# Stick-breaking sums as a VectorE scan, and probabilities and values turned on VectorE and ScalarE

## The chip, the cores and the metric

The kernel runs on one core of a Trainium2 chip. The metric is the device time of one execution in microseconds (us), less being better. The core has a matrix engine (TensorE, PE), two elementwise engines with 128 lanes (VectorE, DVE, and ScalarE, ACT), GpSimd (POOL) and a sync engine (SP) that issues most DMA transfers. Each engine works through its own instructions in a fixed order and waits for the others by semaphores.

## The reference

A two-layer decoder trunk on 272 tokens (16 learned meta tokens and 256 input tokens), 2048 features, 16 heads of 128. Layer 0 is forgetting attention, layer 1 stick-breaking attention; each is followed by a squared-ReLU MLP with 8192 hidden features.

```python
# layer 0, forgetting attention, for a block of queries qs:qe
s = einsum(q[qs:qe], k[:qe]) * scale + cum_logf[q] - cum_logf[k]
p = softmax(where(k_pos <= q_pos, s, -inf))
o = einsum(p, v[:qe])
# layer 1, stick-breaking attention
z = einsum(q[qs:qe], k[:qe]) * scale
mask = k_pos < q_pos
log_beta = log_sigmoid(z)
log_one_minus = where(mask, log_sigmoid(-z), 0.0)
suffix = cumsum(log_one_minus, reverse=True) - log_one_minus
a = where(mask, exp(log_beta + suffix), 0.0)
o = einsum(a, v[:qe])
# both: h = h + o @ w_o ; h = h + square(relu(rms_norm(h) @ w_up)) @ w_down
```

## The kernel before

Activations are feature-major: 16 chunks of 128 features on the partitions, tokens along the free axis. Every matrix product with weights goes through `gemm_group`: 512 output features as four blocks m of 128 with one accumulator each, and four steps kb of 512 input features. Precision comes from splitting: a weight block arrives by DMA in two halves of 128x1024 (`raw`), ACT rounds a half to `whi` (L229), DVE writes the rest to `wlo` (L230), and PE makes three products for each block, hi·hi, lo·hi and hi·lo (L182), 48 matmuls in a kb step. `raw`, `whi` and `wlo` have four buffers each, so that the halves are made up to two kb steps ahead. Steps kb 0 and 3 run block m by block m and read both halves from the start; steps 1 and 2 run half by half.

Each attention works on four groups g of four heads. In layer 0 a group has a q GEMM, a k GEMM, scores and softmax, a v GEMM and outputs; in layer 1 the q GEMMs of all groups come first. Scores are float32 products that PE makes in several passes (`ps` L401; `pza`, `pzb` L579 and L580). In layer 0, queries are on the partitions, so that the probabilities have to be turned before the outputs: PE transposes them (`pp` L432 to L434), DVE copies them. In layer 1, keys are on the partitions, and the running sums over keys are products with triangular and all-ones matrices (`pta`, `ptb` L594 to L599; a corner of 16 queries apart, `pzc`, `ptc`). In both layers PE transposes the values (`token_major`, `pv` L334). The outputs `po` are split into `ao` by ACT and DVE (`put_split`, L355 and L356), which `out_proj` reads.

The program is scheduled: the framework orders each engine's instructions by a simulated timeline, within the data's dependences. Only the order of the GEMM's own matmuls is pinned (`gemm_matmul`).

Of the kernel before, what the change touches and what calls it, by code (L numbers as in the profile page):

```python
# [34 lines left out]
def yoco_kernel(ctx: ExitStack, tc: tile.TileContext, hT_in, gains, b_f, w_f, w_qkv0, w_o0, w_up, w_dn,  # L35
# [25 lines left out]
    for _ in range(9):  # L61
# [15 lines left out]

# [15 lines left out]
    maskB = const.tile([P, 400], F32, name="maskB")  # L93
    nc.gpsimd.memset(maskB, 0.0)
    nc.gpsimd.affine_select(out=maskB[:, 0:256], in_=maskB[:, 0:256], compare_op=ALU.is_gt, fill=-BIG,
                            base=M, pattern=[[1, 256]], channel_multiplier=-1)
    nc.gpsimd.affine_select(out=maskB[:, 256:400], in_=maskB[:, 256:400], compare_op=ALU.is_gt, fill=-BIG,
                            base=0, pattern=[[1, 144]], channel_multiplier=-1)

    maskC = const.tile([P, 4, M], F32, name="maskC")  # L100
    nc.gpsimd.memset(maskC, 0.0)
    nc.gpsimd.affine_select(out=maskC, in_=maskC, compare_op=ALU.is_gt, fill=-BIG, base=M,
                            pattern=[[32, 4], [1, M]], channel_multiplier=-1)
    nc.gpsimd.affine_select(out=maskC, in_=maskC, compare_op=ALU.is_ge, fill=-BIG, base=-M,
                            pattern=[[-32, 4], [0, M]], channel_multiplier=1)
# [9 lines left out]
    pad = align.tile([P, 32], F32, name="pad")  # L115
# [64 lines left out]
    def gemm_matmul(*args, **kw):  # L180

        ins = nc.tensor.matmul(*args, **kw).ins  # L182
# [101 lines left out]
    def load_gates():  # L284
        nc.scalar.dma_start(bf_sb, b_f)

        wf_sb = att.tile([P, NC, NC], F32, tag="v_sb", name="wf_sb")
        wf = att.tile([P, NC, 2 * NC], F32R, tag="v_sb", name="wf")
# [3 lines left out]
        both = att.tile([P, P], F32, tag="pk", name="both")[:2 * NC, :NC]  # L292
# [36 lines left out]
    def token_major(vT, pr, t0, label):  # L329

        pv = patt.tile([P, 2, 2, P], F32, tag="patt", name=f"pv_{label}")
        for i in range(2):
            for b in range(2):
                nc.tensor.transpose(pv[:, i, b, :], vT[:, 2 * pr + i, t0 + b * P:t0 + b * P + P], ident)  # L334
        v_sb = att.tile([P, 2, 2, P], F32, tag="v_sb", name=f"v_sb_{label}")
        nc.scalar.copy(v_sb, pv)
        return v_sb

    def packed(src, label):

        n = src.shape[2]
        t = att.tile([P, P], F32, tag="pk", name=f"pk_{label}")[:, :4 * n]
        nc.gpsimd.tensor_copy(t.rearrange("p (h t) -> p h t", h=4), src)
        return t

    def corners(a, b, label):

        t = att.tile([P, P], F32, tag="pk", name=f"pk_{label}")
# [9 lines left out]
    ao = Split("o0", 0)  # L358
    for g in range(4):
        qT = att.tile([P, 4, T], F32, tag="qT", bufs=4, name=f"qT0_{g}")  # L360
        kT = att.tile([P, 4, T], F32, tag="kT", bufs=1, name=f"kT0_{g}")
        vT = att.tile([P, 4, T], F32, tag="vT", bufs=1, name=f"vT0_{g}")
# [4 lines left out]

        def evac_kv(m, acc, t):
            nc.vector.tensor_tensor(out=t[:, m, :], in0=acc, in1=box["rstd"], op=ALU.mult)
# [14 lines left out]
        s = att.tile([P, 4, 416], F32, tag="s", bufs=1, name=f"s_{g}")  # L384

        def decays(j):

            for i, (o, n) in enumerate(((0, 144), (144, T))):
# [4 lines left out]
        gemm_group(w_qkv0[3 * g + 1], xa, 0, lambda m, acc: evac_kv(m, acc, kT),  # L393
                   after={j: (lambda j=j: decays(j)) for j in range(4)})


        for j in range(4):
            h = 4 * g + j
            ps = patt.tile([P, 512], F32, tag="patt", name=f"ps_{h}")
            for q0, o, n in ((M, 0, 144), (M + P, 144, T)):  # L400
                nc.tensor.matmul(ps[:, o:o + n], qT[:, j, q0:q0 + P], kT[:, j, :n], start=True, stop=True)  # L401
# [13 lines left out]
        s0 = att.tile([P, P], F32, tag="s0", name=f"s0_{g}")  # L415
# [10 lines left out]
        pps = []  # L426
        for pr in range(2):
            pp_sb = att.tile([P, 2, 416], F32, tag="pp", bufs=3, name=f"pp_sb_{g}_{pr}")
            for i in range(2):
                j = 2 * pr + i  # L430
                pp = patt.tile([P, 512], F32, tag="patt", name=f"pp_{4 * g + j}")
                nc.tensor.transpose(pp[:, 0:P], s[:, j, 0:P], ident)  # L432
# [3 lines left out]
            pps.append(pp_sb)  # L436


        pm = patt.tile([P, 512], F32, tag="patt", name=f"pm_{g}")
        nc.tensor.transpose(pm[:, 0:P], corners(s[:, :, P:144], s[:, :, 400:416], f"sm_{g}"), ident)  # L440
        nc.tensor.transpose(pm[:, P:2 * P], s0, ident)
        pm_sb = att.tile([P, 256], F32, tag="pm_sb", bufs=1, name=f"pm_sb_{g}")
        nc.vector.tensor_tensor(out=pm_sb[:, :P].rearrange("p (b q) -> p b q", q=M), in1=maskD, op=ALU.mult,
                                in0=pm[:, P - M:P].unsqueeze(1).to_broadcast([P, 8, M]))
        nc.scalar.copy(pm_sb[:, P:], pm[:, P:2 * P])

        gemm_group(w_qkv0[3 * g + 2], xa, 0, lambda m, acc: evac_kv(m, acc, vT))

        pv = patt.tile([P, 512], F32, tag="patt", name=f"pvm_{g}")
        nc.tensor.transpose(pv[:, :P], packed(vT[:, :, 0:32], f"vm_{g}"), ident)
        nc.tensor.transpose(pv[:, P:2 * P], corners(vT[:, :, P:144], vT[:, :, 256:T], f"vc_{g}"), ident)
        vm_sb = att.tile([P, 2 * P], F32, tag="vm_sb", bufs=1, name=f"vm_sb_{g}")
        nc.scalar.copy(vm_sb, pv[:, :2 * P])
        po = patt.tile([P, 512], F32, tag="patt", name=f"pom_{g}")
        nc.tensor.matmul(po[:, :P], vm_sb[:, :P], pm_sb[:, P:], start=True, stop=True)
        put_split(ao, 4 * g, 4, 0, M, po[:, :P].rearrange("p (h q) -> p h q", h=4)[:, :, :M])
        for pr in range(2):
            v_sb = token_major(vT, pr, 0, f"0_{g}_{pr}")  # L460
            po = patt.tile([P, 2, 256], F32, tag="patt", name=f"po0_{g}_{pr}")
            for i in range(2):
                nc.tensor.matmul(po[:, i, :], v_sb[:, i, 0, :], pps[pr][:, i, 0:2 * P], start=i == 0, stop=False)  # L463
                nc.tensor.matmul(po[:, i, P:], v_sb[:, i, 1, :], pps[pr][:, i, 2 * P:3 * P], start=False, stop=False)  # L464
            nc.tensor.matmul(po.rearrange("p i (c q) -> p (i c) q", c=2)[:, :, P - M:], vm_sb[:, P:],
                             pm_sb[:, 64 * pr:64 * pr + 64], start=False, stop=True)
            put_split(ao, 4 * g + 2 * pr, 2, M, S, po)


    def out_proj(w, ao, t0, gi, label):  # L470
        norm = Norm(label, t0)
        xm = Split(label, t0)
        for g in range(4):
# [5 lines left out]
            gemm_group(w[g], ao, t0, evac, widen=t0 == M)  # L479
# [30 lines left out]
    xm, norm_m = out_proj(w_o0, ao, 0, G_M0, "m0")  # L510
# [30 lines left out]
    ao = Split("o1", M)  # L541
    for g in range(4):
        kT = att.tile([P, 4, T], F32, tag="kT", bufs=1, name=f"kT1_{g}")
        vT = att.tile([P, 4, T], F32, tag="vT", bufs=1, name=f"vT1_{g}")
        gemm_group(w_kv[2 * g], xc, 0, lambda m, acc: evac_kv(m, acc, kT))
        q = qT1[g]

        def softplus(e, z):

            nc.scalar.activation(e, z, AF.Abs)  # L550
            nc.scalar.activation(e, e, AF.Exp, scale=-1.0)
            nc.scalar.activation(e, e, AF.Ln, bias=1.0)
# [179 lines left out]
```

## Time and profile before

| What | Before |
|---|---|
| Time, median of 3 runs | 2303.12 us (2302.21 to 2303.5) |
| Profiled execution, its own time | 2303.47 us |
| Span of the profiled execution | 2301.7 us |
| PE busy | 2290.6 us (100%) |
| DVE busy | 1289.2 us (56%) |
| ACT busy | 1041.2 us (45%) |
| POOL busy | 41.5 us (2%) |
| Attention of layer 0, one group of heads | 80.12 us |
| Attention of layer 1, one group of heads | 56.87 us |

The span runs from the first to the last instruction of the profiled execution; its own time has 1.77 us around the span. A row of a group reads: line, engine, operation, written tile <- read tiles, shapes, count, then busy time, mean ns of one, and idle time just before them with what ended it. A row of a timeline or of the chain starts with start and length in us. A row of a stretch has its bounds, its length, and the busy time and count of each engine.

### The profile page before, as it was taken

What the parts mean: (1) busy time and instruction counts of PE and PEld (TensorE: products, weight loads), DVE (VectorE), ACT (ScalarE), POOL (GpSimd) and SP (SyncE); (2) the same over time, 40 slices, a digit from 0 to 9 for tenths busy, and PEclk for the clock granted to TensorE, in tenths of its full rate; (3) what the DMA queues carried; (4) which work ended last, traced back from release to release, by engine and by line L of the source; (5) the groups of instructions that cost most, each with busy time, mean ns of one, the idle gap of its engine ahead of it and who ended that gap; (6) DMA issues with size and microseconds to landing.
All of it is one profiled execution on the core that took longest, in us unless ns stands there. A gap on an engine that the chain in (4) does not pass through costs nothing.

```text
span 2301.7 us, 44826 instructions
## 1 busy us (share of the span) xinstructions
PE 2290.6 (100%) x19030; PEld 2282.9 (99%) x19030; DVE 1289.2 (56%) x1764; ACT 1041.2 (45%) x1397; POOL 41.5 (2%) x72
## 2 busy tenths in 40 slices
PE   9999999999999999999999999999999999999998
PEld 9999999999999999999999999999999999999998
DVE  7665555655455455455566555566555555555554
ACT  6444344543344344344444444455544543543553
POOL 1000000000000000000000000000000000000000
PEclk9999999999999999999999999999999999999999
DMA  7545555555555555555555544456556566566563
GB/s 235 164 161 173 163 168 166 173 184 172 185 175 176 182 174 184 173 184 174 178 189 186 173 147 147 148 173 201 187 192 201 189 190 203 186 197 199 186 202 129
DMA packets 116904, 412.32 MB, mean 179 GB/s; under 512 B 13520, under 2 KB 16992, under 8 KB 116704
## 3 DMA queue, kind: packets, MB, share of 16 engines
q1 hardware_dynamic: 114560, 406.29, 54.8%
q8 instruction: 149, 2.44, 0.4%
q10 hardware_dynamic: 2144, 3.17, 0.4%
q14 instruction: 51, 0.42, 0.1%
HBM read 407.29 MB, written 2.11 MB: 178 GB/s over the span
## 4 chain that ended last, share of the span: by engine, by line
PE 99%; DMA 1%; DVE 0%; ACT 0%; issue 0%; DVEq 0%; SPq 0%; ACTq 0%
PE acc L182 95%; DMA raw<-w_qkv 1%; PE ps L401 0%; PE pv L334 0%; PE pza L579 0%; PE po L463 0%; PE po L618 0%; PE pzb L580 0%; PE po L619 0%; PE po L464 0%; DMA hT<-hT_in 0%; DVE ob L674 0%; PE pf L301 0%; PE pf L300 0%; PE pta L594 0%; PE pta L595 0%
## 5 line engine op out<-in xcount | busy, mean ns | idle before, releaser
L230 DVE TENSOR_TENSOR wlo<-raw,whi 128x1024 fp32r<-128x1024 f32 (+1 forms) x773 | 929.0, 1218 | 742.7 <-ACT whi L229 736.2
L229 ACT ACTIVATE whi<-raw 128x1024 fp32r<-128x1024 f32 (+1 forms) x773 | 797.3, 1050 | 1010.8 <-PE acc L182 985.9
L182 PE MATMUL acc<-x_m,whi 128*128 128x272 f32 (+1 forms) x4096 | 643.2, 281 | 0.0
L182 PE MATMUL acc<-x_u,whi 128*128 128x272 f32 (+1 forms) x4096 | 642.9, 281 | 0.0
L182 PEld LDWEIGHTS acc<-x_m,whi 128*128 128x128 f32 x4096 | 566.1, 188 | 0.1
L182 PEld LDWEIGHTS acc<-x_u,whi 128*128 128x128 f32 x4096 | 565.9, 188 | 0.0
L182 PE MATMUL acc<-x_m,wlo 128*128 128x272 f32 (+1 forms) x2048 | 440.9, 281 | 0.0
L182 PE MATMUL acc<-x_u,wlo 128*128 128x272 f32 (+1 forms) x2048 | 440.8, 281 | 0.0
L182 PE MATMUL acc<-x_a,whi 128*128 128x272 f32 (+1 forms) x2048 | 360.5, 288 | 0.3 <-ACT whi L229 0.3
L182 PEld LDWEIGHTS acc<-x_m,wlo 128*128 128x128 f32 x2048 | 323.4, 188 | 0.0
L182 PEld LDWEIGHTS acc<-x_u,wlo 128*128 128x128 f32 x2048 | 323.3, 188 | 0.0
L182 PEld LDWEIGHTS acc<-x_a,whi 128*128 128x128 f32 x2048 | 302.3, 189 | 1.8 <-ACT whi L229 0.6
L182 PE MATMUL acc<-x_a,wlo 128*128 128x272 f32 (+1 forms) x1024 | 254.4, 286 | 0.0
L182 PE MATMUL acc<-x_kv,whi 128*128 128x272 f32 x1024 | 191.8, 288 | 0.0
L182 PEld LDWEIGHTS acc<-x_a,wlo 128*128 128x128 f32 x1024 | 175.9, 189 | 1.3 <-issue 0.5
L182 PE MATMUL acc<-x_o,whi 128*128 128x272 f32 (+1 forms) x1024 | 161.9, 282 | 0.0
L182 PEld LDWEIGHTS acc<-x_kv,whi 128*128 128x128 f32 x1024 | 159.7, 188 | 0.0
L182 PE MATMUL acc<-x_kv,wlo 128*128 128x272 f32 x512 | 147.5, 288 | 0.0
L182 PEld LDWEIGHTS acc<-x_o,whi 128*128 128x128 f32 x1024 | 141.7, 188 | 0.0
L259 DVE TENSOR_TENSOR hT<-acc,hT 128x272 f32<-128x272 f32 (+1 forms) x160 | 69.1, 432 | 84.7 <-PE acc L182 84.6
L182 PE MATMUL acc<-x_o,wlo 128*128 128x272 f32 (+1 forms) x512 | 110.5, 282 | 0.0
L182 PEld LDWEIGHTS acc<-x_kv,wlo 128*128 128x128 f32 x512 | 96.4, 188 | 0.0
(225 smaller groups left out, 974.4 us busy)
## 6 DMA issues: line engine op xcount, KB each, us to landing
raw<-w_up SPq DMA_DIRECT2D x256, 512.0 KB, 4.6
raw<-w_dn SPq DMA_DIRECT2D x256, 512.0 KB, 4.6
raw<-w_qkv SPq DMA_DIRECT2D x92, 512.0 KB, 4.0
raw<-w_o SPq DMA_DIRECT2D x64, 512.0 KB, 4.4
raw<-w_kv SPq DMA_DIRECT2D x64, 512.0 KB, 3.8
raw<-w_q SPq DMA_DIRECT2D x32, 512.0 KB, 4.9
fk<-f_dram ACTq DMA_DIRECT2D x4, 544.0 KB, 5.2
raw<-w_qkv SPq DMA_DIRECT2D x7, 256.0 KB, 4.8
```

The lines of the kernel that those rows point to most:

```text
L182: ins = nc.tensor.matmul(*args, **kw).ins
L229: on_act = nc.scalar.activation(hp, src, AF.Copy)
L230: on_dve = nc.vector.tensor_tensor(out=lp, in0=src, in1=hp.bitcast(F32), op=ALU.subtract)
L259: nc.vector.tensor_tensor(out=hT[:, c, t0:], in0=acc, in1=hT[:, c, t0:], op=ALU.add)
```

## The change

Scores of both layers now have queries on the partitions and are made by one function: a float32 product for the first 128 queries (144 keys), and three products of split parts for the other 128 (272 keys); queries are split once per group, keys at each eviction. In layer 1 the sums over keys become DVE scans along the free axis, and the corner is no longer computed apart. Probabilities of both layers are turned by two wide DVE transposes, which turn blocks of 32x32, and sixteen ACT copies that put the blocks in place (`turned`). Values are turned by sixteen DVE transposes of 32 partitions each, which write the blocks in place (`token_major`). The outputs of a group are made later, in two pieces (`late`): in layer 0 ahead of kb 2 of the next q GEMM and after that GEMM; in layer 1 ahead of kb 1 and kb 3 of the next k GEMM; for the last group ahead of kb 1 and kb 3 of `out_proj`'s first GEMM. Some buffers change their pools.

```diff
+    def behind(ins):
+        tc.add_manual_dep(ins.ins, queued[0].name, mybir.DependencyInfo(mybir.DependencyClass.NoSync,
+                                                                        mybir.DependencyReason.DATA))
...
+    def split_q(q, label):
+        parts = [att.tile([P, 4, P], F32R, tag="qs", name=f"q{x}_{label}") for x in ("h", "l")]
+        nc.scalar.activation(parts[0], q, AF.Copy)
+        nc.vector.tensor_tensor(out=parts[1], in0=q, in1=parts[0].bitcast(F32), op=ALU.subtract)
+        return parts
+    def keys(label):
...
+        def evac(m, acc):
+            nc.vector.tensor_tensor(out=kT[:, m, :], in0=acc, in1=box["rstd"], op=ALU.mult)
+            nc.scalar.activation(kh[:, m, :], kT[:, m, :], AF.Copy)
+            nc.vector.tensor_tensor(out=kl[:, m, :], in0=kT[:, m, :], in1=kh[:, m, :].bitcast(F32), op=ALU.subtract)
+    def scores(q, qs, kT, ks, j, label):
+        ps = patt.tile([P, 512], F32, tag="patt", name=f"ps_{label}_{j}")
+        nc.tensor.matmul(ps[:, :144], q[:, j, :], kT[:, j, :144], start=True, stop=True)
+        for i, (a, b) in enumerate(((0, 0), (0, 1), (1, 0))):
+            nc.tensor.matmul(ps[:, 144:416], qs[a][:, j, :], ks[b][:, j, :], start=i == 0, stop=i == 2)
+        return ps
+    def turned(s, label):
...
+        for o, u, n in ((0, 0, P), (144, P, 2 * P)):
+            nc.vector.transpose(out=sb.rearrange("p (h k) -> p h k", h=4)[:, :, u:u + n], in_=s[:, :, o:o + n])
+        sb, out = (t.rearrange("p (u k) -> p u k", k=P) for t in (sb, pt))
+        for a in range(4):
+            for b in range(4):
+                nc.scalar.activation(out[32 * b:32 * b + 32, :, 32 * a:32 * a + 32],
+                                     sb[32 * a:32 * a + 32, :, 32 * b:32 * b + 32], AF.Copy)
-    def token_major(vT, pr, t0, label):
-        pv = patt.tile([P, 2, 2, P], F32, tag="patt", name=f"pv_{label}")
-        for i in range(2):
-            for b in range(2):
-                nc.tensor.transpose(pv[:, i, b, :], vT[:, 2 * pr + i, t0 + b * P:t0 + b * P + P], ident)
-        v_sb = att.tile([P, 2, 2, P], F32, tag="v_sb", name=f"v_sb_{label}")
-        nc.scalar.copy(v_sb, pv)
+    def token_major(vT, label):
+        vt = att.tile([P, 4, T], F32, tag="kv", name=f"vt_{label}")[:, :, :2 * P]
+        out, src = (t.rearrange("p h (b t) -> p h b t", t=P) for t in (vt, vT[:, :, :2 * P]))
+        for a in range(4):
+            for b in range(4):
+                nc.vector.transpose(out=out[32 * b:32 * b + 32, :, :, 32 * a:32 * a + 32],
+                                    in_=src[32 * a:32 * a + 32, :, :, 32 * b:32 * b + 32])
...
@@ layer 0
-            gemm_group(w_qkv0[3 * g], xa, 0, evac_q)
+            gemm_group(w_qkv0[3 * g], xa, 0, evac_q, {2: late[0]})
+        qs = split_q(qT[:, :, M + P:], f"0_{g}")
+        for f in late[1:]:
+            f()
...
-            for i in range(2):
-                j = 2 * pr + i
-                pp = patt.tile([P, 512], F32, tag="patt", name=f"pp_{4 * g + j}")
-                nc.tensor.transpose(pp[:, 0:P], s[:, j, 0:P], ident)
-                nc.tensor.transpose(pp[:, P:2 * P], s[:, j, 144:144 + P], ident)
-                nc.tensor.transpose(pp[:, 2 * P:3 * P], s[:, j, 144 + P:144 + 2 * P], ident)
-                nc.vector.tensor_copy(pp_sb[:, i, :3 * P], pp[:, :3 * P])
+        sm = corners(s[:, :, P:144], s[:, :, 400:416], f"sm_0_{g}")
+        probs = turned(s, f"0_{g}")
+        vT, evac_v = values(f"0_{g}")
+        gemm_group(w_qkv0[3 * g + 2], xa, 0, evac_v)
+        vals = token_major(vT, f"0_{g}")
...
@@ out_proj
-            gemm_group(w[g], ao, t0, evac, widen=t0 == M)
+            gemm_group(w[g], ao, t0, evac, {1: late[0], 3: late[1]} if g == 0 else {}, widen=t0 == M)
...
@@ layer 1
-        gemm_group(w_kv[2 * g], xc, 0, lambda m, acc: evac_kv(m, acc, kT))
+        gemm_group(w_kv[2 * g], xc, 0, evac_k, {1: late[0], 3: late[1]} if late else {})
...
-            nc.tensor.matmul(pa, ntri_r, e_hi[:, :, 0:256], start=True, stop=False)
-            nc.tensor.matmul(pa, ntri_r, e_lo[:, :, 0:256], start=False, stop=False)
-            nc.tensor.matmul(pa[:, :, 112:], nones_r, e_hi[:, :, 256:400], start=False, stop=False)
-            nc.tensor.matmul(pa[:, :, 112:], nones_r, e_lo[:, :, 256:400], start=False, stop=True)
-            nc.tensor.matmul(pb[:, :, :144], ntri_r, e_hi[:, :, 256:400], start=True, stop=False)
-            nc.tensor.matmul(pb[:, :, :144], ntri_r, e_lo[:, :, 256:400], start=False, stop=True)
+            nc.scalar.activation(e[:, two], s[:, two], AF.Abs)
+            nc.scalar.activation(e[:, two], e[:, two], AF.Exp, scale=-1.0)
+            nc.scalar.activation(e[:, two], e[:, two], AF.Ln, bias=1.0)
+            nc.scalar.activation(r[:, two], s[:, two], AF.Relu)
+            for j in range(2 * pr, 2 * pr + 2):
+                for o, n in ((0, 144), (144, T)):
+                    back = slice(o + n - 1, o - 1 if o else None, -1)
+                    nc.vector.tensor_tensor_scan(out=r[:, j, back], data0=r[:, j, back], data1=e[:, j, back],
+                                                 initial=0.0, op0=ALU.add, op1=ALU.add)
+            nc.vector.tensor_tensor(out=r[:, two], in0=s[:, two], in1=r[:, two], op=ALU.subtract)
+            nc.scalar.activation(r[:, two], r[:, two], AF.Exp)
+        probs = turned(r, f"1_{g}")
```

The scheduler sets where the new instructions stand. On DVE, at the end of layer 0's first v GEMM (the third GEMM of the program, `acc_3`), this stood before; `wlo_4_0_0` and `wlo_4_0_1` are the two halves of kb 0 of the GEMM that follows it, and `pp`, `pm` are turned probabilities:

```order
L435 COPY pp_sb_0_1_921<-pp_3_927 128x384
L443 TENSOR_TENSOR pm_sb_0_938<-pm_0_932,maskD_144 128x128
L230 TENSOR_TENSOR wlo_4_0_0_1245<-raw_4_0_0_1240,whi_4_0_0_1244 128x2x512
L230 TENSOR_TENSOR wlo_4_0_1_1249<-raw_4_0_1_1241,whi_4_0_1_1248 128x2x512
L369 TENSOR_TENSOR vT0_0_160<-acc_3_0_941,rstd_a0_561 128x272
L369 TENSOR_TENSOR vT0_0_160<-acc_3_1_942,rstd_a0_561 128x272
L369 TENSOR_TENSOR vT0_0_160<-acc_3_2_943,rstd_a0_561 128x272
L369 TENSOR_TENSOR vT0_0_160<-acc_3_3_944,rstd_a0_561 128x272
L230 TENSOR_TENSOR wlo_4_1_0_1305<-raw_4_1_0_1300,whi_4_1_0_1304 128x2x512
```

And at the same place now, where `sb` are the wide transposes and `vt` the turned values:

```order
L346 STREAM_TRANSPOSE sb_0_0_917<-s_0_583 128x4x128
L346 STREAM_TRANSPOSE sb_0_0_917<-s_0_583 128x4x256
L473 TENSOR_SCALAR s0_0_907<-s0_0_907,st0_0_908 128x128
L215 TENSOR_TENSOR wlo_4_0_0_1219<-raw_4_0_0_1214,whi_4_0_0_1218 128x2x512
L357 TENSOR_TENSOR vT0_0_937<-acc_3_0_938,rstd_a0_542 128x272
L357 TENSOR_TENSOR vT0_0_937<-acc_3_1_939,rstd_a0_542 128x272
L357 TENSOR_TENSOR vT0_0_937<-acc_3_2_940,rstd_a0_542 128x272
L357 TENSOR_TENSOR vT0_0_937<-acc_3_3_941,rstd_a0_542 128x272
L365 STREAM_TRANSPOSE vt_0_0_1191<-vT0_0_937 32x4x2x32 x16
L215 TENSOR_TENSOR wlo_4_0_1_1223<-raw_4_0_1_1215,whi_4_0_1_1222 128x2x512
```

Sixteen turns now stand between the two halves of kb 0, and the second half, which stood ahead of the values' evictions, is behind them. In the other groups of layer 0 the same sixteen stand between the two halves of kb 1 of the following GEMM. In layer 1 they stand ahead of both, as here for its first group (`acc_54` is its v GEMM):

```order
L346 STREAM_TRANSPOSE sb_1_0_14757<-r1_0_14709 128x4x128
L346 STREAM_TRANSPOSE sb_1_0_14757<-r1_0_14709 128x4x256
L215 TENSOR_TENSOR wlo_55_0_1_15063<-raw_55_0_1_15055,whi_55_0_1_15062 128x2x512
L357 TENSOR_TENSOR vT1_0_14777<-acc_54_0_14778,rstd_a1_13533 128x272
L357 TENSOR_TENSOR vT1_0_14777<-acc_54_1_14779,rstd_a1_13533 128x272
L357 TENSOR_TENSOR vT1_0_14777<-acc_54_2_14780,rstd_a1_13533 128x272
L357 TENSOR_TENSOR vT1_0_14777<-acc_54_3_14781,rstd_a1_13533 128x272
L365 STREAM_TRANSPOSE vt_1_0_15029<-vT1_0_14777 32x4x2x32 x16
L215 TENSOR_TENSOR wlo_55_1_0_15126<-raw_55_1_0_15121,whi_55_1_0_15125 128x2x512
L215 TENSOR_TENSOR wlo_55_1_1_15130<-raw_55_1_1_15122,whi_55_1_1_15129 128x2x512
```

On ACT, in the v GEMM of layer 0's second group (`acc_6`), the last two kb steps' halves and the first of the next GEMM stood like this before, with one copy of the turned corner (`pm_sb`) between two of them:

```order
L421 ACTIVATE s0_1_1791,st0_1_1792<-s0_1_1791,st0_1_1792 128x128
L229 ACTIVATE whi_6_2_0_1957<-raw_6_2_0_1953 128x1024
L229 ACTIVATE whi_6_2_1_1961<-raw_6_2_1_1954 128x1024
L229 ACTIVATE whi_6_3_0_2017<-raw_6_3_0_2013 128x1024
L445 COPY pm_sb_1_1826<-pm_1_1820 128x128
L229 ACTIVATE whi_6_3_1_2021<-raw_6_3_1_2014 128x1024
L229 ACTIVATE whi_7_0_0_2132<-raw_7_0_0_2128 128x1024
```

Now the sixteen copies `pt` of the probabilities stand between the two halves of kb 3 (`L457` and `L471` are the softmax's exponentials):

```order
L457 ACTIVATE s_1_1494,st_7_1806<-s_1_1494,st_7_1806 128x144
L457 ACTIVATE s_1_1494,st_7_1806<-s_1_1494,st_7_1806 128x272
L214 ACTIVATE whi_6_2_1_1981<-raw_6_2_1_1974 128x1024
L471 ACTIVATE s0_1_1818,st0_1_1819<-s0_1_1818,st0_1_1819 128x128
L214 ACTIVATE whi_6_3_0_2037<-raw_6_3_0_2033 128x1024
L350 ACTIVATE pt_0_1_1829<-sb_0_1_1828 32x12x32 x16
L214 ACTIVATE whi_6_3_1_2041<-raw_6_3_1_2034 128x1024
```

The second half of kb 3 moved behind the whole block, and the first half of kb 2 ahead of the last head's exponentials.

More of the change, by code (lines that the diff above doesn't have):

```diff
@@ L439, in yoco_kernel @@
[L439 to L467, printed above, removed]
@@ L471, in out_proj @@
+        late = [small, lambda g=g, probs=probs, vals=vals, vm_sb=vm_sb, box=box:
+                outputs(g, ao, probs, vals, box["pm"], vm_sb[:, P:], f"0_{g}")]
+    def out_proj(w, ao, t0, gi, label, late):
         norm = Norm(label, t0)
@@ new lines, in yoco_kernel, with small @@
+        sm = corners(r[:, :, P:144], r[:, :, 400:416], f"sm_1_{g}")
+        probs = turned(r, f"1_{g}")
+        vT, evac_v = values(f"1_{g}")
+        gemm_group(w_kv[2 * g + 1], xc, 0, evac_v)
+        vc = corners(vT[:, :, P:144], vT[:, :, 256:T], f"vc1_{g}")
+        vals = token_major(vT, f"1_{g}")
+        vm_sb = tmp.tile([P, T], F32, tag="relu", name=f"vm1_sb_{g}")[:, :P]
+        def small(g=g, vc=vc, vm_sb=vm_sb, sm=sm, box=box):
+            box["pm"] = corner_probs(sm, f"1_{g}")[1]
+            pv = patt.tile([P, 512], F32, tag="patt", name=f"pvc_{g}")
+            behind(nc.tensor.transpose(pv[:, :P], vc, ident))
+            nc.scalar.copy(vm_sb, pv[:, :P])
@@ L626, in yoco_kernel @@
+        late = [small, lambda g=g, probs=probs, vals=vals, vm_sb=vm_sb, box=box:
+                outputs(g, ao, probs, vals, box["pm"], vm_sb, f"1_{g}")]
+    xm, norm_m = out_proj(w_o1, ao, M, G_M1, "m1", late)
     pms = patt.tile([P, 512], F32, tag="patt", name="pms_fin")
```

177 lines of the change are left out of this document (70 added, 107 removed).

## The prediction

> **What bounds the kernel now.** I read the page's busy times first, then the chain that ended last, then the groups by line, then stretches and timelines of the places where the change works.
>
> ```profile
> PE 2290.6 (100%) x19030; PEld 2282.9 (99%) x19030; DVE 1289.2 (56%) x1764; ACT 1041.2 (45%) x1397; POOL 41.5 (2%) x72
> PE 99%; DMA 1%; DVE 0%; ACT 0%; issue 0%; DVEq 0%; SPq 0%; ACTq 0%
> 441.21 756.83 PE acc L182 x6144
> 141.19:221.31 80.12, 80.12 (x643) 79.60 (x642) 45.96 (x85) 32.28 (x50) 5.37 (x6) 1.00 0.51 165
> ```
>
> The first two rows are the page's: TensorE (PE) is busy all the time and is 99% of the chain. The third is from the chain: 6144 weight-block matmuls in 756.83 us, 0.123 us each, so a kb step of 48 matmuls lasts 5.93 us. The fourth is the stretch of one layer-0 group of heads: length, then PE, weight load, VectorE (DVE) and ScalarE (ACT). PE is busy for all of its 80.12 us, DVE for 45.96. So a microsecond taken off PE is a microsecond gained, as long as the weights' halves arrive; each half has to pass ACT (whi) and then DVE (wlo):
>
> ```profile
> L230 DVE TENSOR_TENSOR wlo<-raw,whi 128x1024 fp32r<-128x1024 f32 x764 | 923.1, 1224 | 739.3 <-ACT whi L229 732.8
> L229 ACT ACTIVATE whi<-raw 128x1024 fp32r<-128x1024 f32 x764 | 792.1, 1056 | 1007.3 <-PE acc L182 985.9 <-issue 7.9 <-ACT sq_m L157 6.4
> 89.49 0.44 DVE L369 TENSOR_TENSOR vT<-acc,rstd_a 128x272 f32<-128x272 f32 x1 [1.04 <-PE acc L182]
> 89.85 2.44 DVE L230 TENSOR_TENSOR wlo<-raw,whi 128x1024 fp32r<-128x1024 f32 x2
> 95.88 2.36 DVE L230 TENSOR_TENSOR wlo<-raw,whi 128x1024 fp32r<-128x1024 f32 x2 [3.58 <-ACT whi L229]
> ```
>
> ACT waits for PE to free a buffer (985.9 of 1007.3 us idle), DVE waits for ACT: the halves run ahead of PE by the four buffers, two kb steps at most. The last three rows are DVE's timeline at the end of a v GEMM. DVE then has 3.58 us to spare in 6 us. A block of work longer than that in its queue, ahead of a wlo, reaches PE.
>
> **What PE is relieved of.**
>
> ```profile
> 63.95 0.70 PE ps L401 x4
> 71.16 0.11 PE pp L432
> 97.19 0.44 PE pv L334 x4
> 1302.58 0.17 PE pzc L557 x2
> 1306.88 0.17 PE ptc L564 x2
> 1307.04 0.22 PE ptc L565 x2
> 1308.00 0.43 PE pza L579 x2
> 1308.43 0.25 PE pzb L580 x2
> 1317.94 0.23 PE pta L594
> 1318.17 0.13 PE ptb L598
> 1319.90 0.23 PE pta L595
> 1320.13 0.14 PE pta L596
> 1320.27 0.13 PE pta L597
> 1320.40 0.13 PE ptb L599
> 78.61 0.11 PE pm L440
> ```
>
> These are pieces of the chain: start, length, tile, matmuls. A head's scores become one float32 product of 144 columns (0.25, as pzb) and three of 272 columns at the GEMM's 0.123: 0.62 instead of 0.70 in layer 0 and 0.68 in layer 1. Per layer-0 group: 4 x 0.08, 12 turned probability tiles at 0.11 and 8 value tiles at 0.11, 2.5 us. Per layer-1 group: 4 x 0.06, the values 0.88, the sums 2 x 0.99, the corner 0.17 + 0.39, less one corner transpose (0.11) that is new, 3.6 us. Four groups each: **24.4 us** less PE work. The late outputs are the same products elsewhere; they cost PE nothing, and remove no wait, since PE had none there.
>
> **The value turns.** Sixteen DVE instructions per group, each 32 partitions x 256 elements, stand in DVE's queue between two wlo's, as the order above shows. No row of before is a turn. Nearest rows:
>
> ```profile
> L499 DVE TENSOR_TENSOR x_u<-u,x_u 128x256 fp32r<-128x256 f32 x64 | 25.4, 417 | 0.0
> 145.03 0.16 DVE L409 RECIPROCAL st<-st 128x2 f32<-128x2 f32 x1
> 145.22 0.56 DVE L411 TENSOR_SCALAR s<-s,st 128x144 f32<-128x144 f32 x2
> ```
>
> 256 float32 elements take 0.417. Independent instructions overlap: in the earlier timeline the wlo starts 0.36 after a vT of 0.44, so a turn could cost 0.417 - 0.08 = 0.33. An instruction that has to wait for the one before starts 0.03 after its end (145.19 to 145.22): 0.45. I take 0.45, because a block must be collected before it can leave turned, and each of these writes other partitions than the last; 16 x 0.45 = 7.2 us.
>
> [...]
>
> With T the end of the v GEMM on PE, the last vT ends at T + 0.44.
> - Layer 0, first group: the second half of the *next* kb 0 is behind the turns: T + 0.44 + 7.2 + 1.22 = T + 8.9. kb 0 runs m by m and wants it after 8 matmuls, T + 1.0. PE stands **7.9 us**.
> - Layer 0, other three: one wlo (pitch 1.13) is ahead, and the half behind the turns is kb 1's second, ready at T + 10.0, wanted at T + 5.93 + 2.97 + 0.25 = T + 9.15: 0.85 each, **2.6 us**.
> - Layer 1, three groups: behind stands kb 1's first half, ready T + 8.9, wanted at T + 6.4 with two small transposes ahead: 2.45 each. In the last group the next GEMM is out_proj, which uses wlo 16 matmuls later: about 1.1. **8.5 us**.
>
> **The probability copies.** Sixteen ACT instructions of 32 x 384 per group.
>
> ```profile
> L157 ACT ACTIVATE sq_a<-hT 128x272 f32<-128x272 f32 x30 | 12.0, 417 | 0.2 <-DVE wlo L230 0.2
> L550 ACT ACTIVATE e<-z 128x800 f32<-128x800 f32 x8 | 7.0, 872 | 21.6 <-DVE z L583 21.6
> 94.78 2.01 ACT L229 ACTIVATE whi<-raw 128x1024 fp32r<-128x1024 f32 x2 [0.37 <-PE acc L182]
> L603 DVE TENSOR_TENSOR z<-pta,z 128x512 f32<-128x512 f32 x8 | 5.5, 692 | 7.9 <-PE pta L597 7.9
> 149.46 0.56 DVE L411 TENSOR_SCALAR s<-s,st 128x144 f32<-128x144 f32 x2
> ```
>
> Between 0.417 at 272 and 0.872 at 800 elements, 384 take 0.51; two whi's of 1.06 take 2.01, an overlap of 0.1, so 0.41 per copy and 6.6 us per block. In layer 0, groups 2 to 4, they stand between the two halves of the v GEMM's kb 3. In before the last probabilities were ready 8.8 us after the k GEMM's end (141.19 to 150.02). Add the two wlo's now ahead (2.4), the two wide turns (0.69 for 512 elements, 1.22 for 1024) and about 1.4 of waiting for whi's: 14.5. Copies to 21.1, whi 22.2, wlo 23.5; PE wants it after the scores (2.5), the rest (0.3), three kb steps and 8 matmuls, 21.4. 2.1 each, **6.3 us**. In the first group and in layer 1 the copies stand ahead of a half that is not wanted for some 2 us more, or that waits for the turns anyway: nothing; that cover goes if a copy takes over 0.54.
>
> The scans and wide ACT steps of layer 1 lie under the v GEMM's 23.7 us and feed only work that is now late: nothing.
>
> **Outputs and the clock.**
>
> ```profile
> L356 DVE TENSOR_TENSOR x_o<-po,x_o 128x512 fp32r<-128x512 f32 x16 | 11.0, 690 | 15.2 <-ACT x_o L355 15.2
> L355 ACT ACTIVATE x_o<-po 128x512 fp32r<-128x512 f32 x16 | 9.5, 595 | 22.7 <-PE po L465 17.2 <-PE po L620 5.5
> L62 PE MATMUL idle<-mean_w 128*128 128x128 f32 x18 | 4.2, 430 | 1.1 <-DVE mean_w L58 1.1
> 3.63 1.70 PE L62 MATMUL idle<-mean_w 128*128 128x128 f32 x7
> 7.08 0.34 PE L182 MATMUL acc<-x_a,wlo 128*128 128x272 f32 x1
> L432 PE MATMUL pp<-ident,s 128*128 128x128 f32 x16 | 4.3, 271 | 0.0
> ```
>
> In out_proj the last group's outputs stand directly ahead of the kb 3 that reads them: 0.60 + 0.69 less the six matmuls of kb 3 that come before the part so made (0.74), 0.55 for each layer, **1.0 us**. PE's first matmuls run slower (0.430 against 0.271 for 128 columns), from 3.63 until about 7.08 us. After the 7.9 us stand I expect that again: 3.4 us at about half rate, **1.7 us**; and **1 us** for restarts after some ten stalls. [...]
>
> **Sum.** 7.9 + 2.6 + 8.5 + 6.3 + 1.0 + 1.7 + 1.0 = 29.0 us of standing against 24.4 saved: +4.6 on the profiled execution's 2303.47, which is 0.35 above the median, so 2307.7 against 2303.12: **2308.0 us**. Each 0.01 us on a value turn moves this by 1.3 us.
>
> **Rivals.**
> - *The turns overlap* (0.33 each). The first stall falls to 6.0, the layer-0 others to nothing, layer 1 to 0.55 three times; with 6.3 + 1.0 + 2.7 that is 17.7, a net of -6.7: **2296 us**. For it: overlapping rows everywhere on DVE. Against it: all those write the same partitions as their neighbour. Chance 0.22.
> - *The quarter-width copies and turns don't overlap and cost more*: copies 0.535, turns 0.50. The copies add 2.0 in three groups and use up layer 1's cover, the turns 0.8 in eight places: +12.4, **2320 us**. It decides from 0.54 a copy. For it: each instruction changes partitions on both sides. Chance 0.16, slower.
> - *Turns of 4-byte words run at half rate*, as the scan does:
>
> ```profile
> L318 DVE TENSOR_TENSOR_SCAN fc<-fx,fe 16x272 f32<-16x272 f32 x1 | 0.7, 712 | 0.0
> ```
>
>   At 0.72 each a block is 4.3 us longer, in eight places: **2342 us**. Only the scan is that slow. Chance 0.08.
> - *The stalls are absorbed*: if the scheduler's order is not what the engines meet (weights' halves further ahead than I count), only the saving is left, at best 2279. The rows of wlo that wait for ACT speak against it, ACT's for PE: nothing can run further ahead. Chance 0.03.
>
> **Numbers.** The forecast has 0.51, and its own spread (stalls +-6) reaches from 2302 to 2314. Range 2292 to 2325: it takes in the first two rivals, and leaves out the last two and the tails. A difference of 0.2%, 4.6 us, is about what can be told here. Faster: the overlapping turns, the absorbed stalls and a little of the forecast's own spread, 0.27. Within 0.2%: not quite half the forecast's, 0.22. Slower: 0.51.
>
> **What would show it.** A group of DVE turns with a mean near 0.42 to 0.48 and no overlap; PE idle named after DVE wlo for about 8 us once in layer 0, under 1 us three times there, near 2.5 us three times in layer 1; PE idle near 2 us in the v GEMM's kb 3 of three groups, behind ACT whi or DVE wlo; PE's busy time 24 us lower. Wrong would be: PE idle under 15 us in all, or stalls at places that this text doesn't name, above all in the k GEMMs of layer 1.

## The result, and the profile after

The changed kernel takes 2319.93 us (median of 4 runs, 2317.48 to 2322.66) against 2302.66 us before (2302.16 to 2303.5): a ratio of 1.0075, 95% interval 1.0057 to 1.0092. It is slower by 17 us where 5 us were forecast. The profiled execution took 2322.33 us, its span is 2320.6 us, 18.9 longer than before's.

The page's first row and the chain:

```profile
PE 2280.8 (98%) x18882; PEld 2272.9 (98%) x18882; DVE 1359.6 (59%) x1909; ACT 1110.3 (48%) x1533; POOL 27.5 (1%) x75
PE 92%; DVE 2%; ACT 1%; issue 1%; DVEq 0%; ACTq 0%
PE acc L162 90%; DVE vt L365 1%; ACT pt L350 1%; DVE wlo L215 1%; PE po L384 1%; PE ps L338 0%; PE po L387 0%; PE ps L336 0%; DVE sb L346 0%; ACT whi L214 0%; PE po L388 0%; DVE ob L668 0%; DVE vT L357 0%; PE pms_fin L625 0%; DVE ob L665 0%
```

PE was 99% of the chain and is 92%; the value turns (`vt`), the copies (`pt`) and some `wlo` have come into it. What PE waited for (in total, times, longest):

```profile
PE acc L162 <- DVE wlo L215: 19.5, 11, 5.7
PE acc L162 <- ACT whi L214: 8.8, 5, 2.2
```

Before had one such wait, of 0.3 us. The first place that the prediction named, the end of layer 0's first v GEMM, on DVE, ACT and PE:

```profile
85.73 0.44 DVE L357 TENSOR_TENSOR vT<-acc,rstd_a 128x272 f32<-128x272 f32 x1 [1.04 <-PE acc L162]
86.21 7.18 DVE L365 STREAM_TRANSPOSE vt<-vT 32x256 f32<-32x256 f32 x16
93.42 3.50 DVE L215 TENSOR_TENSOR wlo<-raw,whi 128x1024 fp32r<-128x1024 f32 x3
78.85 8.53 ACT L350 ACTIVATE pt<-sb 32x384 f32<-32x384 f32 x16 [1.01 <-DVE sb L346]
87.40 2.95 ACT L214 ACTIVATE whi<-raw 128x1024 fp32r<-128x1024 f32 x3
88.51 0.51 PE L162 MATMUL acc<-x_a,whi 128*128 128x272 f32 x2 [2.08 <-ACT whi L214]
94.70 0.60 PE L162 MATMUL acc<-x_a,wlo 128*128 128x272 f32 x1 [5.67 <-DVE wlo L215]
```

Sixteen turns last 7.18 us without a gap, the wlo follows, and PE stands for 2.08 + 5.67 us. The first 2.08 us go to the whi behind ACT's sixteen copies, but the wlo of the same half, behind the turns, comes later still, so that the copies add nothing here. The other two places that it named, the v GEMM's kb 3 of layer 0's second group and the k GEMM's kb 1 behind layer 1's first group:

```profile
160.56 8.53 ACT L350 ACTIVATE pt<-sb 32x384 f32<-32x384 f32 x16 [1.15 <-DVE st L472]
170.23 0.82 PE L162 MATMUL acc<-x_a,whi 128*128 128x272 f32 x2 [2.17 <-ACT whi L214]
1344.51 7.18 DVE L365 STREAM_TRANSPOSE vt<-vT 32x256 f32<-32x256 f32 x16
1353.00 0.40 PE L162 MATMUL acc<-x_kv,wlo 128*128 128x272 f32 x1 [2.69 <-DVE wlo L215]
```

The mean lengths, by group:

```profile
L350 ACT ACTIVATE pt<-sb 32x384 f32<-32x384 f32 x128 | 66.9, 522 | 8.9 <-DVE sb L346 4.0 <-DVE st L472 3.4
L365 DVE STREAM_TRANSPOSE vt<-vT 32x256 f32<-32x256 f32 x128 | 55.8, 436 | 2.1
```

What the prediction counted once happens at many stalls. These are stretches of 3.41 us (start and end, length, PE, weight load, DVE, ACT and POOL busy; the third number from the end is the granted clock, as a share of full speed):

```profile
166.74:170.15 3.41, 1.32 (x11) 1.10 (x9) 0.00 (x0) 3.34 (x7) 0.00 (x0) 1.00 0.00 0
170.15:173.56 3.41, 2.90 (x11) 2.58 (x12) 3.35 (x3) 1.92 (x3) 0.00 (x0) 0.50 0.29 89
173.56:176.98 3.42, 3.42 (x17) 3.42 (x17) 0.93 (x3) 0.00 (x0) 0.00 (x0) 0.50 0.81 264
1351.28:1354.69 3.41, 1.69 (x13) 1.69 (x14) 3.38 (x5) 1.09 (x2) 0.00 (x0) 1.00 0.18 52
1463.90:1467.30 3.40, 0.72 (x6) 0.52 (x5) 3.33 (x6) 2.26 (x4) 0.00 (x0) 0.99 0.00 0
1467.30:1470.70 3.40, 3.40 (x17) 3.40 (x17) 3.02 (x4) 0.00 (x0) 0.00 (x0) 0.51 0.79 241
```

In the first stretch PE stands for 2.1 us in a v GEMM of layer 0; the clock then is 0.50 for two stretches, in which PE does 11 and 17 matmuls instead of some 28. Summed over stretches of 0.5 us, PE in both attentions and in the out_proj after them is idle for 28.8 us, and loses about 12 us more at a clock of 0.50 (PE busy there, times the share by which a matmul's 0.123 us falls short of the 0.226 seen there).

### The profile page after: what moved, and what is told of

Read it like the earlier page. It is cut to its first block, busy times and chain, and to the rows that moved or that the text cites. A ratio compares the mean times of both kernels' runs of the same rounds, so it can differ in the third digit from the quotient of the medians.

```text
span 2320.6 us, 44744 instructions
## 1 busy us (share of the span) xinstructions
PE 2280.8 (98%) x18882; PEld 2272.9 (98%) x18882; DVE 1359.6 (59%) x1909; ACT 1110.3 (48%) x1533; POOL 27.5 (1%) x75
## 4 chain that ended last, share of the span: by engine, by line
PE 92%; DVE 2%; ACT 1%; issue 1%; DVEq 0%; ACTq 0%
PE acc L162 90%; DVE vt L365 1%; ACT pt L350 1%; DVE wlo L215 1%; PE po L384 1%; PE ps L338 0%; PE po L387 0%; PE ps L336 0%; DVE sb L346 0%; ACT whi L214 0%; PE po L388 0%; DVE ob L668 0%; DVE vT L357 0%; PE pms_fin L625 0%; DVE ob L665 0%
## 5 line engine op out<-in xcount | busy, mean ns | idle before, releaser
L162 PEld LDWEIGHTS acc<-x_a,whi 128*128 128x128 f32 x2048 | 307.9, 193 | 10.1 <-ACT whi L214 9.9
```

## The experiments

**The same instructions in other places (spread turns and copies).** Turns and copies become functions that the GEMMs call behind their halves:

```diff
-                nc.vector.transpose(out=out[32 * b:32 * b + 32, :, :, 32 * a:32 * a + 32],
-                                    in_=src[32 * a:32 * a + 32, :, :, 32 * b:32 * b + 32])
+        def turns(lo, hi):
+            for a, b in [(a, b) for a in range(4) for b in range(4)][lo:hi]:
+                nc.vector.transpose(out=out[32 * b:32 * b + 32, :, :, 32 * a:32 * a + 32],
+                                    in_=src[32 * a:32 * a + 32, :, :, 32 * b:32 * b + 32])
+    def spread(copies, turns):
+        def step(kb):
+            copies(kb + 1)
+            turns(*((0, 4), (4, 10), (10, 16))[kb])
+        return {kb: (lambda kb=kb: step(kb)) for kb in range(3)}
...
-        gemm_group(w_qkv0[3 * g + 2], xa, 0, evac_v)
+        gemm_group(w_qkv0[3 * g + 2], xa, 0, evac_v, after={3: lambda: copies(0)})
-            gemm_group(w_qkv0[3 * g], xa, 0, evac_q, {2: late[0]})
+            gemm_group(w_qkv0[3 * g], xa, 0, evac_q, {2: late[0]}, after=later)
```

> The same instructions as the changed kernel, but the sixteen value turns stand as 4 + 6 + 6 behind the weights' halves of kb 0, 1 and 2 of the GEMM that follows, and the sixteen copies as 4 behind the halves of the v GEMM's kb 3 and 4 behind each of kb 0, 1, 2. Theory (the blocks stand ahead of weights' halves; PE idle 28.8 us and 13 us of half rate come from that, and PE is saved 23 us): no stall over 0.5 us but for the outputs in the two out_proj, no half rate, 2302.7 - 23 + 1 = 2281 us. Rival (the amount of added DVE and ACT work costs, wherever it stands): 2312 to 2320 us.

Measured: 2279.05 us, ratio to before 0.9900 (0.9885 to 0.9914). DVE's timeline at the same place, and the page's first row:

```profile
86.60 0.44 DVE L359 TENSOR_TENSOR vT<-acc,rstd_a 128x272 f32<-128x272 f32 x1 [1.04 <-PE acc L162]
86.96 1.22 DVE L215 TENSOR_TENSOR wlo<-raw,whi 128x1024 fp32r<-128x1024 f32 x1
88.09 1.78 DVE L368 STREAM_TRANSPOSE vt<-vT 32x256 f32<-32x256 f32 x4
89.90 1.23 DVE L215 TENSOR_TENSOR wlo<-raw,whi 128x1024 fp32r<-128x1024 f32 x1
91.16 2.68 DVE L368 STREAM_TRANSPOSE vt<-vT 32x256 f32<-32x256 f32 x6
PE 2265.8 (99%) x18882; PEld 2260.6 (99%) x18882; DVE 1360.1 (60%) x1909; ACT 1111.4 (49%) x1533; POOL 29.8 (1%) x75
```

DVE and ACT do as much as in the changed kernel (1360.1 against 1359.6 us), and all waits of PE on weights' halves are gone. The same work costs 41 us less in other places; the rival that the amount counts falls.

**Both kinds of turns on PE again.** `turned` becomes twelve PE transposes and four DVE copies, `token_major` eight PE transposes and two ACT copies; the rest stays.

```diff
-        for o, u, n in ((0, 0, P), (144, P, 2 * P)):
-            nc.vector.transpose(out=sb.rearrange("p (h k) -> p h k", h=4)[:, :, u:u + n], in_=s[:, :, o:o + n])
...
+        for j in range(4):
+            pp = patt.tile([P, 512], F32, tag="patt", name=f"pp_{label}_{j}")
+            for i, o in enumerate((0, 144, 144 + P)):
+                nc.tensor.transpose(pp[:, i * P:i * P + P], s[:, j, o:o + P], ident)
+            nc.vector.tensor_copy(pt[:, j, :], pp[:, :3 * P])
...
-                nc.vector.transpose(out=out[32 * b:32 * b + 32, :, :, 32 * a:32 * a + 32],
-                                    in_=src[32 * a:32 * a + 32, :, :, 32 * b:32 * b + 32])
+                    nc.tensor.transpose(pv[:, i, b, :], vT[:, 2 * pr + i, b * P:b * P + P], ident)
+            nc.scalar.copy(vt[:, 2 * pr:2 * pr + 2], pv)
```

> Values and probabilities turned on PE again, in both layers; scores, scan and late outputs as in the changed kernel. PE gets 8 + 12 transposes of 0.11 us per group back, 17.6 us in eight groups. Theory of the blocks: 41.9 us of waits and half rate go, 2319.9 + 17.6 - 41 = 2296 to 2298 us. Rival (the late outputs, the key splits or the scan cause part of the stalls): stalls stay, 2305 us or more.

Measured: 2296.98 us, 0.9979 (0.9970 to 0.9988), as expected. Late outputs, splits and scans stall nothing but the 0.7 us of waits for `x_o` in the two out_proj.

**Only the values on PE.** The second half of that diff.

> Only the values turned on PE again. +7.0 us of PE work. Theory of the blocks: the stalls behind the turns go (7.75 us in the first group falls to about 3.2, because the copies stand ahead of the same half; three of 1.0, three of 2.7, one of 1.5), and with them the half rate in layer 1 (3.4 us): 2304 to 2308 us, with three stalls of 2.6 us and their half rate left in layer 0. Rival (only the one long stall matters): 2315 us.

Measured: 2302.40 us, 1.0000 (0.9990 to 1.0009), 2 us below the range. Its ten executions spread from 2299.40 to 2304.72 us, the profiled one is the slowest. PE still waited in layer 0, for the copies:

```profile
PE acc L162 <- ACT whi L214: 8.1, 5, 2.2
PE acc L162 <- DVE wlo L215: 3.0, 4, 0.7
```

In the profiled execution 11.1 us of waits (0.4 of them at the program's start) and about 6 of half rate are left, the second less than I had counted; the ten executions were granted 0.998 of the full clock at 2299.40 us down to 0.995 at 2304.72, so most of them had less of it. The first group stands for 1.9 us behind the copies, which the turns had covered.

**Only the probabilities on PE.** The first half of that diff.

> Only the probabilities turned on PE again. +10.6 us of PE work. Theory of the blocks: three stalls of 2.6 us and about 7 us of half rate in layer 0 go, the first group's stall stays at 7.7 us because the turns hold it up anyway: 2319.9 + 10.6 - 7.8 - 7 = 2315 to 2317 us. Rival (the half rate is not caused by these stalls): 2322 us or more.

Measured: 2297.26 us, 0.9979 (0.9970 to 0.9989): 18 us below the range. The turns are unchanged, but the long stall isn't there:

```profile
89.84 1.21 DVE L215 TENSOR_TENSOR wlo<-raw,whi 128x1024 fp32r<-128x1024 f32 x1
90.97 7.17 DVE L363 STREAM_TRANSPOSE vt<-vT 32x256 f32<-32x256 f32 x16
98.18 4.63 DVE L215 TENSOR_TENSOR wlo<-raw,whi 128x1024 fp32r<-128x1024 f32 x4
99.46 0.39 PE L162 MATMUL acc<-x_a,wlo 128*128 128x272 f32 x1 [0.89 <-DVE wlo L215]
```

Without the copies on ACT the scheduler orders DVE anew: in all eight groups the turns now stand between kb 1's two halves, so that PE waits 0.9 us at most, and the execution was granted 0.998 of the full clock, as before's was, against the changed kernel's 0.991. The block's length is the same, 7.17 us. The long stall was there only with the copies in place. The expectation took the order as given.

**Idle products where PE stands.**

```diff
+    def warm(n):
+        pw = patt.tile([P, 512], F32, tag="patt", name=f"warm_{uid[0]}")
+        for _ in range(n):
+            ins = nc.tensor.transpose(pw[:, :P], ident, ident).ins
+            tc.add_manual_dep(ins, queued[0].name, mybir.DependencyInfo(mybir.DependencyClass.NoSync,
+                                                                        mybir.DependencyReason.DATA))
+            queued[:] = [ins]
...
+            gemm_group(w_qkv0[3 * g], xa, 0, evac_q, {0: lambda: warm(62), 2: late[0]} if g == 1 else {2: late[0]})
```

> The changed kernel with idle products put into PE's queue where it stands: 62 transposes of the identity (0.11 us each) ahead of kb 0 of layer 0's second q GEMM, 20 ahead of kb 3 of the v GEMM in its groups 2 to 4, 21 ahead of kb 1 of the k GEMM in layer 1's groups 2 to 4. They fill most of each stall and feed nothing. Theory (the stalls let the clock fall to half rate, 13 us): PE still starts its real work at the same times, the granted clock stays at 1.00 in all these places, and the time falls by 10 to 13 us, to 2307 to 2310 us. Rival (the lost time is the waiting alone, the half rate costs nothing since PE would wait for DVE and ACT later anyway): no change or up to 3 us more than the changed kernel.

Measured: 2311.17 us (2310.10 to 2311.91), 8.8 below the changed kernel, or 7.9 when each is set against the before measured beside it; 2307 to 2310 was expected. At the first and second stall:

```profile
86.00:98.00 12.00, 10.76 (x94) 10.54 (x94) 10.92 (x20) 5.18 (x8) 0.65 (x3) 1.00 0.10 25
160.00:176.00 16.00, 15.26 (x124) 14.84 (x123) 5.80 (x9) 12.00 (x20) 0.00 (x0) 1.00 0.42 128
```

The clock stays at 1.00. PE does more work and the program ends earlier: the half rate is a cost of its own, 8 to 9 us of it shown directly by the times. From the start of the first norm's product (`pms_a`) to that of the last norm's (`pms_fin`) the profile takes 2254.1 us against the changed kernel's 2265.5: 11.4 us, close to the 12 counted above.

**Turns and copies that stay on their partitions.**

```diff
-                nc.vector.transpose(out=out[32 * b:32 * b + 32, :, :, 32 * a:32 * a + 32],
+                nc.vector.transpose(out=out[32 * a:32 * a + 32, :, :, 32 * b:32 * b + 32],
...
-                nc.scalar.activation(out[32 * b:32 * b + 32, :, 32 * a:32 * a + 32],
+                nc.scalar.activation(out[32 * a:32 * a + 32, :, 32 * b:32 * b + 32],
```

> Every turn and every copy writes the same 32 partitions that it reads (the blocks stay where they are, so the probabilities and values are not whole transposes); four in a row have the same partitions. Theory (an instruction that changes partitions waits until the one before has ended): turns in a row start 0.36 us apart instead of 0.45, copies 0.43 instead of 0.53, except one in four. Rival (turns and copies of a quarter never overlap): 0.45 and 0.53 as before.

Measured once: 2298.70 us, for a kernel whose blocks are not put in place.

```profile
86.59 5.71 DVE L365 STREAM_TRANSPOSE vt<-vT 32x256 f32<-32x256 f32 x16
79.24 7.09 ACT L350 ACTIVATE pt<-sb 32x384 f32<-32x384 f32 x16 [1.01 <-DVE sb L346]
```

Sixteen turns in 5.71 us instead of 7.18 (0.36 each for 0.45), sixteen copies in 7.09 instead of 8.53, as the next experiment's first row has them (0.44 each for 0.53). A turn lasts 0.404 us on the mean here and a copy 0.510 (0.436 and 0.522 in the changed kernel), so that in this run, where the partitions stay, the instructions of both engines overlap, by some 0.05 and 0.07 us.

**Whole blocks, placed later.** The turns as one block behind kb 1's halves, the copies behind the v GEMM's kb 3; against the spread kernel:

```diff
-        return {kb: (lambda kb=kb: step(kb)) for kb in range(3)}
+        return {1: lambda: turns(0, 16)}
...
-        gemm_group(w_qkv0[3 * g + 2], xa, 0, evac_v, after={3: lambda: copies(0)})
+        gemm_group(w_qkv0[3 * g + 2], xa, 0, evac_v, after={3: lambda: [copies(a) for a in range(4)]})
```

> The blocks stay whole, sixteen in a row, but stand later: the value turns behind both weights' halves of kb 1 of the GEMM that follows, the copies behind both halves of the v GEMM's kb 3. Theory (the place counts, not the length: a block behind kb 1's halves has until kb 2): no stall behind the turns; one of 2 to 3 us in layer 0's first group, where the copies still stand ahead of the next GEMM's second half, with or without 1.7 us of half rate after it: 2281 to 2284 us. Rival (sixteen in a row are too long wherever they stand): 2290 us or more.

Measured: 2310.33 us, 1.0037 (1.0025 to 1.0050): the theory that only the place counts fell. Layer 0 went as expected, with one stall of 2.8 us. In layer 1 (ACT, DVE, PE):

```profile
1316.26 8.53 ACT L351 ACTIVATE pt<-sb 32x384 f32<-32x384 f32 x16 [0.80 <-DVE sb L346]
1325.91 2.36 DVE L215 TENSOR_TENSOR wlo<-raw,whi 128x1024 fp32r<-128x1024 f32 x2 [5.02 <-ACT whi L214]
1328.19 4.91 DVE L368 STREAM_TRANSPOSE vt<-vT 32x256 f32<-32x256 f32 x11
1336.97 0.50 PE L162 MATMUL acc<-x_kv,wlo 128*128 128x272 f32 x1 [3.59 <-DVE wlo L215]
```

ACT's block holds up kb 1's whi, kb 1's wlo waits 5.02 us for it, and DVE's block, placed behind that wlo, starts late by as much: the two blocks come one after the other, 8.5 and 7.5 us. PE waits 3.59 us, in each of four groups about as long, and at three of the four the granted clock falls to 0.50; the execution was granted 0.993. The small pieces of the spread kernel avoid that (0.998); a late place alone doesn't.

**Scores in float32, with the spread.**

```diff
-        for i, (a, b) in enumerate(((0, 0), (0, 1), (1, 0))):
-            nc.tensor.matmul(ps[:, 144:416], qs[a][:, j, :], ks[b][:, j, :], start=i == 0, stop=i == 2)
+        nc.tensor.matmul(ps[:, 144:416], qs[:, j, :], kT[:, j, :], start=True, stop=True)
```

> The kernel with the spread turns and copies, but the scores of the second 128 queries as one float32 product (0.45 us) instead of three of split parts (0.37), and no splits of queries and keys. Theory: PE does 32 x 0.08 = 2.6 us more and nothing else changes: 2281 to 2282 us. Rival (the splits' ACT and DVE work costs as much as it gains): 2279 us.

Measured: 2281.94 us, 0.9912 (0.9897 to 0.9927), 2.9 above the spread kernel. The split scores are worth their splits.

**Last outputs a step earlier, with the spread.** For the last group, also 8 + 8 turns behind kb 0 and kb 1:

```diff
-            gemm_group(w[g], ao, t0, evac, {1: late[0], 3: late[1]} if g == 0 else {},
+            gemm_group(w[g], ao, t0, evac, {1: late[0], 2: late[1]} if g == 0 else {},
```

> The kernel with the spread turns and copies; in the two out_proj the last group's turns and copies are done by kb 1 and its outputs stand ahead of kb 2 instead of kb 3. Theory: the two waits for x_o (0.4 and 0.3 to 0.4 us) go: 2278.3 us. Rival (blocks of eight turns make a new stall): 2279 us or more.

Measured: 2276.74 us, 0.9889 (0.9875 to 0.9904), the fastest version. Both waits for `x_o` are gone. It gains 2.3 us over the spread kernel where 0.8 were counted. By the starts of the norms' products in the two profiles, 1.5 us of it lie in the attentions and 0.9 ahead of the first norm, at 36.9 us instead of 37.8. That start lies anywhere between 36.9 and 39.3 us in this study's profiles, before's at 38.7; the 0.7 us more in the attentions are not explained.

**The changed kernel twice more.**

> The changed kernel again, unedited, for a second profile of it. Theory (the clock is judged in fixed windows of 3.41 us that do not start with the program, so the same stall falls into one window or is shared by two): the same stalls, 28 to 29 us of PE idle, but another set of them followed by half rate; time = 2279.5 + idle - 0.8 + loss, between 2315 and 2323 us. Rival (a stall of 2.6 us always or never costs its half rate, by its length): the same six places at half rate and 2322 us, within 0.5 us.

> The changed kernel once more, a third profile, expected as the second: the same stalls, and half rate after four to seven of them, not all the same as in the other two profiles; 2315 to 2323 us. Rival: the same six places, 2322 us.

Measured: 2320.87 and 2322.70 us. PE is idle for 28.7 and 28.8 us, stall by stall as in the first profile within 0.2 us. Of the second profile:

```profile
1348.50:1351.50 3.00, 0.31 (x3) 0.09 (x2) 2.93 (x6) 2.31 (x4) 0.00 (x0) 1.00 0.00 0
1351.50:1355.00 3.50, 3.50 (x20) 3.50 (x21) 3.48 (x4) 0.00 (x0) 0.00 (x0) 0.66 0.72 201
1464.00:1467.00 3.00, 0.31 (x4) 0.09 (x2) 2.93 (x6) 2.37 (x4) 0.00 (x0) 1.00 0.00 0
1467.00:1470.50 3.50, 3.50 (x28) 3.50 (x29) 3.50 (x4) 0.00 (x0) 0.00 (x0) 1.00 0.64 206
```

Here layer 1's first stall is followed by a slow clock and the third is not, the reverse of the first profile, with 2.69 us each in both. So length alone didn't decide here. With the values on PE, too, layer 0 has three stalls of 2.9 us, and only the first two are followed by half rate, while one of 1.9 us is. The third profile has the six places of the first, as the rival of its expectation had it; its stalls lie within 0.1 us of where the first one's lie on the grid described at the end. The times of unedited runs spread over 5 us (2317.5 to 2322.7) where those of the warm kernel spread over 1.8. The two runs at 2317.5 were granted 0.993 of the full clock, those at 2322.3 and 2322.7 were granted 0.991; 0.002 of the time is 4.6 us, so the half rate would account for the spread, though no profile of the faster two was taken.

## Why the prediction was right or wrong

The direction was right, slower, for the reason given: blocks of turns and copies ahead of weights' halves cost PE more than it was relieved of. The size was too small by 14 us in the profiled execution (+18.9 against +4.6). The forecast's own spread, 2302 to 2314, missed the time; the range held it because it took in the second rival, and that is luck in part, as the copies show below. (The sum gives 2307.7 for the median; 2308.0 belongs to the profiled execution.) Term by term:

- *PE's saving, 24.4 us:* right. The spread kernel gains 23.0 us with about 0.8 of waits left, and its PE is busy for 24.8 us less than before's. The sign that the text gave, PE's busy time 24 us lower, did not show in the changed kernel: it fell by 9.8, as matmuls at half rate are busy for longer (one in 0.226 us instead of 0.123).
- *Value turns, 0.45 each:* right, 7.18 us for sixteen: they don't overlap (0.436 us on the mean, 0.45 apart). Of the two reasons given for 0.45, a run bears out the change of partitions: with the blocks left on their partitions the turns overlap, 0.404 us each and 0.36 apart. That a block must be collected first was an assumption of mine, and did not keep those apart.
- *The long stall, 7.9:* 2.08 + 5.67 = 7.75. *The others of layer 0, 2.6:* 2.3. *Layer 1, 8.5:* three of 2.7 and one of 1.5, 9.6.
- *Copies, 6.3:* three stalls of 2.6 to 2.9, 8.4. The working slipped a little: its own terms give a half ready at 23.4 and wanted at 21.6, so 1.8 each and 5.4. The step "an overlap of 0.1, so 0.41 per copy" was wrong: they start 0.53 apart, as the second rival had it. That rival's number, 2320 us, is the measured one, but by luck and not for its reason: it added 12.4 us of waiting, and only about 2 came from there.
- *Outputs, 1.0:* 0.7.
- *The clock, 1.7 us:* this term failed. The loss behind the long stall was about right (3.8 us of PE's work at half rate, 1.7 us), but I applied it to that stall alone. The 3.4 us and the half rate were an estimate from the program's start; in the first profile the granted clock stays at 0.50 for 6.83 us three times and for 3.41 us three times. It falls at stalls of 2.6 to 2.9 us as well: of the thirteen stalls in the first profile the long one and five of the six of 2.6 to 2.9 us, about 12 us in all. The warm kernel takes 8 to 9 us of that away although its stalls hold PE's useful work up as before.
- *Restarts, 1 us:* an estimate that no run shows apart; between the same two scores of layer 0 the changed kernel needs 7.1 us more than the spread one, of which waits and half rate make about 6.3. From the first norm's product to the last norm's it is 44.1 us, of which waits make 28.1 and half rate 12. Some 2.5 of the 4 us left may be the way that idle time is counted (an estimate): a matmul's record lasts 0.29 us where one starts every 0.12, so each of the 15 gaps reads some 0.17 short. The rest is open.

The rival of overlapping turns and that of turns at half rate fell with the 0.436 us row, that of absorbed stalls with the 28.8 us that PE stood. What the prediction took as fixed, and the runs did not, is the order: with the copies gone, the long stall was gone too.

## What to carry to other kernels

Where TensorE is the bound and its weights are prepared by two other engines, each with a few buffers of lead, the question for every instruction added there is not how much it adds but how long a run of them stands ahead of the next half; split such runs into pieces shorter than the spare time of one step, on each of the two engines (here pieces of 1.8 to 2.7 us on DVE, with 3.58 us to spare in 6: 2279 us instead of 2320). Price a TensorE stall not at its length alone: here the long stall and most of those of 1.9 to 3.6 us were followed by 3.41 or 6.83 us at a clock of 0.50, which cost 1.4 to 2.9 us each in the first profile (an estimate: 46% of PE's 3.14 to 6.32 us of work there, at 0.226 us a matmul instead of 0.123); one stall of 2.69 us was followed by it in one profile and not in the next. And read the order again after each edit, since the scheduler may move a block that was not touched.

## What the runs showed of the hardware

- The granted clock changed on a grid of 3.413 us that does not start with the program. In the changed kernel's first profile it falls at 91.64, 170.15, 255.48, 340.82, 1409.19 and 1467.22 us; these times lie 23, 25, 25, 313 and 17 times 3.413 us apart within 0.2 us, and it stays at 0.50 for 6.83 us after the first three and for 3.41 after the others. Four falls of the second profile, near 171.6, 256.95, 1352.6 and 1410.65 us (from the clock's mean in stretches of 0.5 us), lie 25, 321 and 17 such steps apart, but 1.4 to 1.5 us beside the first one's grid. In the first profile, in the stretch of the grid ahead of each of the six falls, PE was busy for 0.51 to 1.32 us, so that a stretch need not be idle throughout for the clock to fall; one with 1.57 was not followed by half rate. What decides within a stretch was not shown. At half rate 2.90 us of work did not bring the full clock back in the first profile, while 3.14 did there and 2.88 in the second; and at the end of the program, where many products have a single column, half rate followed 2.01 us of work, so PE's busy time is not the measure itself:

```profile
88.23:91.64 3.41, 0.51 (x2) 0.30 (x2) 3.30 (x9) 2.12 (x3) 0.00 (x0) 1.00 0.00 0
1351.16:1354.57 3.41, 1.57 (x12) 1.57 (x13) 3.37 (x6) 1.21 (x3) 0.00 (x0) 1.00 0.14 40
340.82:344.23 3.41, 3.14 (x14) 3.14 (x15) 2.84 (x4) 0.85 (x1) 0.00 (x0) 0.50 0.56 179
256.95:260.36 3.41, 2.88 (x12) 2.88 (x13) 3.10 (x4) 1.12 (x2) 0.00 (x0) 0.50 0.52 167
2306.90:2310.30 3.40, 2.01 (x18) 1.84 (x16) 0.95 (x5) 0.82 (x3) 0.00 (x0) 1.00 0.00 0
```

- Sixteen ScalarE copies of 32 partitions x 384 values in a row, each writing other partitions than the one before, did not overlap: 0.52 us long, they start 0.53 us apart. Where three in four stay on the partitions of the one before, they start 0.44 us apart, at 0.51 us each.
- A DVE transpose of 32 partitions x 256 float32 values took 0.436 us, of 128 x 1024 values 1.2 us: about as long as elementwise work of the same width here (0.417 and 1.22 us).
